# One gate pair computed plain inside the attention stage, attention operands formed three heads ahead, z's splits moved, scores and bias table negated

## The chip, the cores and the metric

The kernel runs on one core of a Trainium2 chip, in one launch. Its work is spread over TensorE (PE, matmuls into PSUM), VectorE (DVE), ScalarE (ACT), GpSimd (POOL) and SyncE (SP, which issues most DMAs); each engine takes its instructions in a fixed order, and waits on semaphores where it needs another's result. The metric is the device time of one execution in microseconds, the median over runs. Before the change it is 641.82 us (640.44 to 642.54 in 3 runs).

## The reference

One decoder layer on 512 tokens of 1024 channels, all in float32: a combined projection, a block-sparse attention with 8 heads of 64 channels and a bias by distance, a pooling mixer beside it, both merged by sigmoid gates, an output projection, a layer norm, a gated MLP with a short convolution, and another layer norm. The parts that the change touches:

```python
proj = h @ w_in[l]
q, k, v, p, g = jnp.split(proj, [ATTN_WIDTH, 2 * ATTN_WIDTH, 3 * ATTN_WIDTH, 3 * ATTN_WIDTH + POOL_WIDTH], axis=-1)
y_attn = moba_attention(q.reshape(hs), k.reshape(hs), v.reshape(hs), rel_bias) @ w_branch_attn[l]
y_pool = multiscale_pool(p, w_pool_group[l], pool_scale[l]) @ w_branch_pool[l]
gates = jax.nn.sigmoid(g.astype(jnp.float32)).astype(h.dtype).reshape(B, S, N_BRANCHES, D)
mixed = gates[:, :, 0] * y_attn + gates[:, :, 1] * y_pool
...
s_own = jnp.einsum('hqd,hkd->hqk', qc, k_own).astype(jnp.float32) * scale
s_own = jnp.where((d_own >= 0)[None], s_own + bias_own, NEG)
...
p = jax.nn.softmax(logits, axis=-1).astype(v.dtype)
```

With 512 tokens and blocks of 256 every block is chosen, so the attention is plain causal attention.

## The kernel before

*Products.* A float32 product is made of three matmuls on operands that are split in two rounded parts: high x high, high x low, low x high (L249). `split` (L73) makes the high part on ScalarE (L77) and the low part on VectorE (L78). Weights come as chunks of 128 x 1024 by DMA on SyncE (`fetch`, L138) and are split into a ring of five slots; `state["limit"]` says how far the fetching may run ahead.

*Pairs of tiles by seven products.* Two output tiles of 128 channels that share their input are computed by a scheme with seven block products instead of eight (`seven`, L296). Its weight chunks are A, X, D and Y, of which X and Y are sums: X is formed by a DMA that adds in memory (L201), Y on VectorE (L215). The last product of a pair (`close`, L313) is put off until the next pair runs `flush`. In this way are made the pool projection and the four q/k pairs (key "i", 0 to 4), the eight gate pairs (key "g", one tile for each branch) and most of the MLP (key "f"). A tile made without it, by 24 matmuls of 512 columns, is called plain here (`in_tile`, L490).

*Attention.* `head(h)` (L436) forms a head's operands: a copy of k and of q with their rounding remainders on ScalarE and VectorE, and then SyncE sends the two k tiles to the other half of the partitions (L453, tiles k and kl). `scores(h)` (L535) multiplies them (tile sc, L546 and L547), adds the bias strip and takes the running maximum on VectorE (L550, a reduction into nm), negates nm (L553), exponentiates on ScalarE (L556), and multiplies by the reciprocal of the sums on GpSimd (L561). `trans(h)` (L622) transposes the probabilities on TensorE (tile tr) and copies them out of PSUM, and `pv(p)` (L637) multiplies two heads with v (tile ob). The bias strips are read from a table in memory that `make_table` (L383) and `write_end` (L403) fill.

*Fillers.* Between the steps of the heads TensorE does the products of the pool branch, br with z as input: `br_mm(h, 1)` in the loop over heads (L654 to L667), one for each of heads 0 to 6. They need z's splits (L651), which stand ahead of the loop. `head(h + 3)` is put behind the softmax of head h + 1. Then come the products of the attention branch (`BR0`), the eight gate pairs (L732), which `gate_done` multiplies into the branch products, and the output projection.

*Order.* The order within each engine is made by a scheduler when the program is built, from the order of the code and estimates; `tc.issue_after(ins)` puts what is written under it behind `ins` on that instruction's own engine, and on no other. PSUM has eight banks, each reused when its last reader has run.

## Time and profile before

| | before |
|---|---|
| median of 3 runs | 641.82 us (640.44 to 642.54) |
| profiled execution | 642.55 us |
| its span, first to last instruction | 640.5 us |
| mean granted TensorE clock | 0.985 |
| attention stage (first scores to the last value product) | about 76 to 161 us |
| gate pairs | 174 us to about 252 us |

The span is what the trace covers; 2.05 us of the profiled execution lie around it. In the views that follow, a row of a timeline has the start and the length in us, the engine, the line of the kernel, the operation, the tile written and the tiles read (without their numbers), and in brackets the idle time of that engine ahead of it with what ended it. The letters in tile names: sa, sb and sc with i, g or f are the PSUM banks of a seven-product pair; sc alone is a head's scores; whi and wlo are the two parts of a weight chunk. A matmul's length overlaps with the next one's start, so the distance of two starts tells its cost. A row of waits has engine, line and tile, what was waited for, and the us in total, the times and the longest.

### The profile page before, as it was taken

How to read it: one execution, taken by the hardware profiler on the slowest of the kernel's cores; microseconds unless marked ns; L12 is line 12 of the kernel's file. 1: busy time of each engine (PE TensorE's matmuls, PEld its weight loads, DVE VectorE, ACT ScalarE, POOL GpSimd, SP SyncE). 2: the span in 40 equal slices, each digit the busy share in tenths (PEclk: the TensorE clock that was granted, in tenths of full speed). 3: DMA queues.
4: the chain of work that ended last, by engine and by line, in shares of the span. 5: the costliest groups of instructions: out<-in, count | busy, mean ns of one | idle time of the engine just before them, and what ended most of it. 6: DMA issues, size and time to landing. Idle time of an engine off the chain costs nothing.

```text
span 640.5 us, 10780 instructions
## 1 busy us (share of the span) xinstructions
PE 622.2 (97%) x4132; PEld 560.3 (87%) x4132; DVE 518.0 (81%) x800; ACT 364.9 (57%) x560; POOL 117.7 (18%) x131
## 2 busy tenths in 40 slices
PE   9999989889999999999999999999999999999994
PEld 6899978666899999888999999999999888888884
DVE  6978778563779998749898888899897959698596
ACT  6646667563566565604576666567656447555352
POOL 0133133433012211210102010111100202123202
PEclk9999997889999999999999999999999999999998
DMA  8567645335377844551828877777753995899905
GB/s 315 157 187 185 173 124 166 99 98 165 99 211 183 212 119 131 178 218 45 252 84 203 192 197 197 173 194 198 185 141 117 324 271 118 207 205 201 267 2 131
DMA packets 44259, 110.87 MB, mean 173 GB/s; under 512 B 4512, under 2 KB 6824, under 8 KB 43952
## 3 DMA queue, kind: packets, MB, share of 16 engines
q1 hardware_dynamic: 30464, 75.05, 35.0%
q0 software_dynamic: 13168, 34.10, 28.5%
q10 hardware_dynamic: 576, 1.05, 0.4%
q8 instruction: 32, 0.52, 0.3%
q14 instruction: 19, 0.16, 0.1%
HBM read 104.91 MB, written 3.17 MB: 169 GB/s over the span
## 4 chain that ended last, share of the span: by engine, by line
PE 90%; DMA 5%; DVE 2%; ACT 1%; issue 1%; SPq 0%; DVEq 0%; ACTq 0%; POOLq 0%
PE saf L255 5%; PE saf L251 5%; PE saf L254 5%; PE v L428 3%; PE fi L251 3%; PE fi L254 3%; PE fi L255 3%; PE sbf L255 2%; PE sbf L251 2%; PE sbf L254 2%; PE sag L251 2%; PE wo L255 2%; PE wo L254 2%; PE wo L251 2%; PE sag L254 2%; PE sag L255 2%
## 5 line engine op out<-in xcount | busy, mean ns | idle before, releaser
L78 DVE TENSOR_TENSOR wlo<-araw,whi 128x1024 fp32r<-128x1024 f32 x60 | 72.8, 1222 | 6.7 <-ACT whi L77 6.0
L77 ACT ACTIVATE whi<-araw 128x1024 fp32r<-128x1024 f32 x60 | 62.7, 1057 | 20.4 <-PE sag L254 6.2
L77 ACT ACTIVATE whi<-wraw 128x1024 fp32r<-128x1024 f32 (+1 forms) x45 | 45.1, 1016 | 38.8 <-DMA wraw<-in_w_fo 10.9
L78 DVE TENSOR_TENSOR wlo<-wraw,whi 128x1024 fp32r<-128x1024 f32 (+1 forms) x45 | 53.3, 1192 | 16.8 <-ACT whi L77 16.6
L201 POOL DMA_DIRECT2D xraw<-in_w_fi x15 | 18.0, 1203 | 137.4 <-DMA xraw<-in_w_fi 54.4
L77 ACT ACTIVATE whi<-tw 128x1024 fp32r<-128x1024 f32 (+1 forms) x30 | 29.4, 983 | 23.5 <-DMA tw<-in_w_fo 10.4
L78 DVE TENSOR_TENSOR wlo<-tw,whi 128x1024 fp32r<-128x1024 f32 (+1 forms) x30 | 33.3, 1125 | 7.1 <-ACT whi L77 7.1
L255 PE MATMUL sbf<-T_hi,wlo 128*128 128x256 f32 x136 | 37.9, 279 | 0.0
L251 PE MATMUL saf<-hT_hi,whi 128*128 128x256 f32 x136 | 37.8, 278 | 0.0
L255 PE MATMUL saf<-nT_hi,wlo 128*128 128x256 f32 x136 | 37.8, 278 | 0.0
L254 PE MATMUL saf<-nT_lo,whi 128*128 128x256 f32 x136 | 37.8, 278 | 0.0
L251 PE MATMUL sbf<-T_hi,whi 128*128 128x256 f32 x136 | 37.7, 278 | 0.0
L254 PE MATMUL sbf<-T_lo,whi 128*128 128x256 f32 x136 | 37.7, 277 | 0.0
L254 PE MATMUL saf<-hT_lo,whi 128*128 128x256 f32 x136 | 37.7, 277 | 0.0
L251 PE MATMUL saf<-nT_hi,whi 128*128 128x256 f32 x136 | 37.7, 277 | 0.0
L255 PE MATMUL saf<-hT_hi,wlo 128*128 128x256 f32 x136 | 37.7, 278 | 0.0
L251 PE MATMUL fi<-hT_hi,whi 128*128 128x256 f32 (+1 forms) x112 | 36.2, 328 | 0.2 <-ACT hT_hi L77 0.2
L254 PE MATMUL fi<-hT_lo,whi 128*128 128x256 f32 (+1 forms) x112 | 36.4, 327 | 0.0
L255 PE MATMUL fi<-hT_hi,wlo 128*128 128x256 f32 (+1 forms) x112 | 36.3, 326 | 0.0
L561 POOL TENSOR_SCALAR pp<-pp,rs 128x128 f32<-128x128 f32 (+3 forms) x32 | 24.6, 784 | 23.0 <-DVE rs L558 19.0
L239 POOL DMA_DIRECT2D tw<-in_w_fo x18 | 15.6, 895 | 59.8 <-DVE wlo L78 59.8
L254 PEld LDWEIGHTS saf<-hT_lo,whi 128*128 128x128 f32 x136 | 25.5, 188 | 0.0
(338 smaller groups left out, 2249.9 us busy)
## 6 DMA issues: line engine op xcount, KB each, us to landing
tw<-in_w_fo POOLq DMA_DIRECT2D x20, 512.0 KB, 8.9
araw<-in_w_fi SPq DMA_DIRECT2D x17, 512.0 KB, 3.9
xraw<-in_w_fi SPq DMA_DIRECT2D x15, 512.0 KB, 4.3
xraw<-in_w_fi POOLq DMA_DIRECT2D x15, 512.0 KB, 6.6
araw<-in_w_c SPq DMA_DIRECT2D x13, 512.0 KB, 4.3
wraw<-in_w_fi SPq DMA_DIRECT2D x10, 512.0 KB, 4.4
wraw<-in_w_fo SPq DMA_DIRECT2D x10, 512.0 KB, 6.9
tw<-in_w_fo SPq DMA_DIRECT2D x10, 512.0 KB, 7.7
```

The lines of the kernel that those rows point to most:

```text
L77: state["hi"] = nc.scalar.activation(hi, src, AF.Copy)
L78: state["lo"] = nc.vector.tensor_tensor(lo, src, hi.bitcast(F32), op=ALU.subtract)
L201: state["acc"] = nc.gpsimd.dma_start(v, bass.AP(tensor=a.tensor, offset=a.offset, ap=[[pst, pn], [u.offset + S - a.offset, 2], [est, S]]), ...
L239: nc.gpsimd.dma_start(raw, half(then[1:], sl), accum_op=ALU.add)
L251: ins = nc.tensor.matmul(out_, wh, ah, start=start, stop=False, **kw)
L254: nc.tensor.matmul(out_, wh, al, start=False, stop=False, **kw)
L255: nc.tensor.matmul(out_, wl, ah, start=False, stop=stop, **kw)
L428: nc.tensor.matmul(bs[j], xs_[j][a], (wh, wl)[b], start=kt == 0 and n == 0, stop=False)
L561: nc.gpsimd.tensor_scalar(pp[:, offs[i]:offs[i] + n], pp[:, offs[i]:offs[i] + n], rs[:, i:i + 1], 1.0, op0=ALU.mult, op1=ALU.mult)
```

## The change

It does five things.

1. Gate pair 0 is no longer made by seven products. Its two tiles (g0 and g8) are plain, and they are made inside the attention loop, as the fillers of heads 0 and 1. VectorE copies them to a buffer `plain_gate`; their sigmoids, the multiplication with the branch products and the sum stand behind the first remaining gate pair.
2. The br products with z move back by two heads: filler h is br product h - 2, and one more filler stands behind the last head.
3. `head(h + 3)` is put behind the softmax of head h (of head 1 for the first), not of head h + 1.
4. z's splits move from ahead of the loop to behind head 0's round, and are held until the softmax of head 1.
5. The table of biases and its end are negated and k isn't, so that PSUM holds the scores with their sign turned: VectorE takes a minimum, which is the bias that the exponential needs, and the negation of nm falls away; the exponential gets a scale of -1.

```diff
-    for f in range(KT):
+    for j in (0, KT):
+        add(("g", j), w_c[first["g"] + j])
...
+    for f in range(1, KT):
         add_seven(("g", f), w_c[first["g"] + f], w_c[first["g"] + KT + f])
...
-            nc.vector.tensor_copy(F_sb[:H, S - lo_ - n:S - lo_],
-                                  bass.AP(tensor=rel.tensor, offset=at_, ap=[[pst, pn], [step, n]]))
+            nc.vector.tensor_scalar(F_sb[:H, S - lo_ - n:S - lo_],
+                                    bass.AP(tensor=rel.tensor, offset=at_, ap=[[pst, pn], [step, n]]), -1.0, None,
+                                    op0=ALU.mult)
...
-        nc.vector.memset(neg[:H, :STRIP - S], NEG)
+        nc.vector.memset(neg[:H, :STRIP - S], -NEG)
...
-            nc.scalar.activation(K1[h][own, :], kb[own, :], AF.Copy, scale=-1.0)
-            nc.vector.scalar_tensor_tensor(KL[h][own, :], kb[own, :], -1.0, K1[h][own, :].bitcast(F32),
-                                           op0=ALU.mult, op1=ALU.subtract)
+            nc.scalar.activation(K1[h][own, :], kb[own, :], AF.Copy)
+            nc.vector.tensor_tensor(KL[h][own, :], kb[own, :], K1[h][own, :].bitcast(F32), op=ALU.subtract)
...
-    state["limit"] = at["br", (2, 1)][0]
+    state["limit"] = at["g", KT]
...
-            nc.vector.tensor_tensor_reduce(out=pp[:, offs[i]:offs[i] + n], in0=dst[i][:, :n],
-                                           in1=strips[h][:, S - n:], scale=1.0, scalar=-3.0e38,
-                                           op0=ALU.add, op1=ALU.max, accum_out=nm[:, i:i + 1])
-        nms[h] = nc.vector.tensor_scalar(nm, nm, -1.0, None, op0=ALU.mult)
+            nms[h] = nc.vector.tensor_tensor_reduce(out=pp[:, offs[i]:offs[i] + n], in0=dst[i][:, :n],
+                                                    in1=strips[h][:, S - n:], scale=1.0, scalar=3.0e38,
+                                                    op0=ALU.add, op1=ALU.min, accum_out=nm[:, i:i + 1])
...
-                                           bias=nm[:, i:i + 1], accum_out=rs[:, i:i + 1])
+                                           scale=-1.0, bias=nm[:, i:i + 1], accum_out=rs[:, i:i + 1])
...
+    plain_gate = keep.tile([P, 2, S], F32, name="plain_gate")
...
-    for k in range(4):
-        split(zT_hi[:, k, :], zT_lo[:, k, :], zT[:, k, :])
-    turned = state["hi"].ins, state["lo"].ins
+
+    def cover(h):
+        if h < 2:
+            nc.vector.tensor_copy(plain_gate[:, h, :], in_tile("g", h * KT))
+        else:
+            f = h - 2
+            state["limit"] = at["br", (min(f + 3, KT - 2), 1)][0]
+            with tc.issue_after(turned[0]), tc.issue_after(turned[1]):
+                br_done(f, 1, br_mm(f, 1))
+
     for h in range(H):
         if h + 3 < H:
-            head(h + 3, nms[h + 1], exps[h + 1])
-        if h < KT - 1:
-            state["limit"] = at["br", (min(h + 3, KT - 2), 1)][0]
-            with tc.issue_after(turned[0]), tc.issue_after(turned[1]):
-                br_done(h, 1, br_mm(h, 1))
+            head(h + 3, nms[max(h, 1)], exps[max(h, 1)])
+        cover(h)
         if h + 2 < H:
             scores(h + 2)
...
             trans(h)
+        if h == 0:
+            state["limit"] = at["br", (2, 1)][0]
+            with tc.issue_after(nms[1].ins), tc.issue_after(exps[1].ins):
+                for k in range(4):
+                    split(zT_hi[:, k, :], zT_lo[:, k, :], zT[:, k, :])
+            turned = state["hi"].ins, state["lo"].ins
+    cover(H)
...
-    for f in range(KT):
+    for f in range(1, KT):
...
+        if f == 1:
+            with tc.issue_after(state["add"].ins):
+                for br in range(2):
+                    nc.scalar.activation(plain_gate[:, br, :], plain_gate[:, br, :], AF.Sigmoid)
+                    nc.vector.tensor_tensor(branch[0, br], branch[0, br], plain_gate[:, br, :], op=ALU.mult)
+            merged(0, branch[0, 0], branch[0, 1])
```

The rest of the diff swaps which of two buffers an even and an odd gate pair use.

What the scheduler makes of it stands in the order of the instructions. First TensorE around the first transposes of head 0, before (sai4 is the last q/k pair, br0_1 the first br product with z, sc2 the scores of head 2):

```order
L255 MATMUL sai4_968<-xT_hi_73,wlo25_973 128x256
L251 MATMUL br0_1_1163<-zT_hi_1086,whi26_1017 128x512
L546 MATMUL sc2_01_1182<-k1_2_1138,q1_2_1137 128x256
L547 MATMUL sc2_01_1182<-kl_2_1139,q1_2_1137 128x256
...
L547 MATMUL sc2_3_1184<-kl_2_1139,q1_2_1137 128x512
L630 MATMUL tr0_0_1208<-ident_174,pp0_939 128x128 x4
L630 MATMUL tr0_1_1209<-ident_174,pp0_939 128x128 x4
L630 MATMUL tr0_2_1210<-ident_174,pp0_939 128x128 x2
L254 MATMUL br0_1_1163<-zT_lo_1087,whi26_1017 128x512
```

and TensorE at the same transposes of the change (g8 is the second plain gate tile):

```order
L257 MATMUL sai4_967<-inT1_hi_89,wlo23_871 128x256
L549 MATMUL sc2_3_1187<-kl_2_1138,q1_2_1136 128x512
L632 MATMUL tr0_0_1210<-ident_174,pp0_939 128x128 x4
L632 MATMUL tr0_1_1211<-ident_174,pp0_939 128x128 x4
L632 MATMUL tr0_2_1212<-ident_174,pp0_939 128x128 x2
L253 MATMUL g8_1255<-xT_hi_73,whi27_1035 128x512
L256 MATMUL g8_1255<-xT_lo_74,whi27_1035 128x512
```

Before the transposes the whole last pair has run, and a br product with z stands around them; now the second gate follows, and the last part of the last pair (its close) comes behind 23 of that gate's 24 matmuls.

Second, VectorE from the weight chunk ahead of head 3's operands on, in the change (kl and q1 are a head's operands, pp with nm a reduction of its scores, rk3 and sai4 the additions that end the last q/k pair):

```order
L78 TENSOR_TENSOR wlo28_1245<-wraw28_1243,whi28_1244 128x1024
L308 TENSOR_TENSOR rk3_966<-rk3_966,sbi4_1000 128x256
L559 RECIPROCAL rs1_1097<-rs1_1097 128x4
L450 TENSOR_TENSOR kl_3_1147<-rk1_666,k1_3_1146 64x512
L452 SCALAR_TENSOR_TENSOR q1_3_1145<-rq1_851,q1_3_1145 64x4x128
L450 TENSOR_TENSOR kl_4_1236<-rk2_804,k1_4_1235 64x512
L452 SCALAR_TENSOR_TENSOR q1_4_1234<-rq2_1013,q1_4_1234 64x4x128
L552 ISA pp2_1182,nm2_1183<-sc2_01_1185,strip2_937 128x128
L552 ISA nm2_1183 128x1
L552 ISA pp2_1182,nm2_1183<-sc2_01_1185,strip2_937 128x256
```

Before, head 4's two rows stood behind the reductions of head 3, and the additions into sai4 stood ahead of head 3's operands; now head 4's rows are ahead of the reductions of head 2, and those additions follow behind them.

Third, ScalarE between the exponentials of heads 2 and 3, in the change (zT_hi are z's splits, PT0 and PT1 the copies of transposed probabilities, L754 the sigmoids of the plain gates):

```order
L634 ACTIVATE PT0_1209<-tr0_0_1210 128x512
L77 ACTIVATE zT_hi_1085<-zT_78 128x512 x4
L77 ACTIVATE whi30_1417<-wraw30_1416 128x1024
L754 ACT_TABLE_LOAD
L754 ACTIVATE plain_gate_1089<-plain_gate_1089 128x512
L77 ACTIVATE whi31_1561<-wraw31_1560 128x1024
L77 ACTIVATE whi32_1712<-wraw32_1711 128x1024
L529 ACTIVATE rq3_1134<-sai4_967 128x512
L754 ACTIVATE plain_gate_1089<-plain_gate_1089 128x512
L634 ACTIVATE PT1_1310<-tr1_0_1311 128x512
L557 ACT_TABLE_LOAD
L557 ACTIVATE pp3_1283,rs3_1285<-pp3_1283,nm3_1284 128x128
```

Before, z's splits stood ahead of the exponentials of head 2, and no table load stood in the attention stage behind the one for the first exponential; now the two sigmoids, each table loaded anew, are ahead of the exponentials of head 3.

## The prediction, made before the changed kernel was run

> **What bounds the kernel now.** I read the page first, then TensorE's waits, its timeline at those waits, and last the granted clock around them.

> ```profile
> span 640.5 us, 10780 instructions
> ...
> PE 622.2 (97%) x4132; PEld 560.3 (87%) x4132; DVE 518.0 (81%) x800; ACT 364.9 (57%) x560; POOL 117.7 (18%) x131
> ...
> PEclk9999997889999999999999999999999999999998
> ```

> TensorE is busy for 97% of the span, so a change pays only by less TensorE work, fewer of its waits, or a higher clock. A slice of the clock strip is 16 us long: the 7, 8, 8 are slices 7 to 9, from 96 to 144 us, the attention stage. What stands still there, the list of TensorE's waits tells:

> ```profile
> PE sc L546 <- DMA k<-k: 4.1, 2, 2.1
> PE sai L251 <- DVE sai L311: 2.4, 1, 2.4
> ...
> PE br L251 <- ACT zT_hi L77: 1.2, 1, 1.2
> PE sag L251 <- ACT quad L304: 0.4, 1, 0.4
> ```

> The timeline of TensorE places them; the bracket is the idle time ahead of a row:

> ```profile
> 94.91 0.39 PE L251 MATMUL sai<-xT_hi,whi 128*128 128x256 f32 x1 [2.39 <-DVE sai L311]
> ...
> 98.27 0.79 PE L251 MATMUL br<-zT_hi,whi 128*128 128x512 f32 x1 [1.18 <-ACT zT_hi L77]
> ...
> 115.65 0.77 PE L546 MATMUL sc<-k,q 128*128 128x256 f32 x3 [2.10 <-DMA k<-k]
> ...
> 132.29 0.76 PE L546 MATMUL sc<-k,q 128*128 128x256 f32 x3 [1.99 <-DMA k<-k]
> ```

> The sum is 2.39 + 1.18 + 2.10 + 1.99 = 7.66 us. The last close of the q/k projections waits for VectorE, the first filler product waits for z's splits, and the scores of heads 4 and 6 wait for the copy of k into the other half of the partitions. A wait costs more than its length, as the windows behind each show (length, TensorE busy, granted clock):

> ```profile
> 94.90:103.30 8.40, 7.22 (x33) 0.59 0.41 111
> 115.60:121.20 5.60, 5.55 (x27) 0.70 0.46 141
> 132.20:138.20 6.00, 5.91 (x29) 0.72 0.23 51
> 140.00:190.00 50.00, 50.00 (x309) 1.00 0.54 150
> ```

> The clock is halved for a while, and then full again. Lost are 8.40 x 0.41 = 3.44, less half of the 1.18 us that were idle anyway (0.59), so 2.85; then 5.60 x 0.30 = 1.68 and 6.00 x 0.28 = 1.68: together **6.2 us**. [...]

> **The change, part by part.** *Work on TensorE.* Gate pair 0 loses its seven products (84 matmuls of 256 columns) and gets two plain tiles (2 x 24 of 512). Three starts in a row of full-clock work:

> ```profile
> 171.50 0.39 PE L251 MATMUL br<-oT_hi,whi 128*128 128x512 f32 x1
> ...
> 174.22 0.28 PE L251 MATMUL sag<-xT_hi,whi 128*128 128x256 f32 x1
> ...
> 177.00 0.28 PE L251 MATMUL sbg<-gT_hi,whi 128*128 128x256 f32 x1
> ```

> 12 matmuls of 512 columns start from 171.50 to 174.22, 0.2267 each; 24 of 256 from there to 177.00, 0.1158 each. 48 x 0.2267 - 84 x 0.1158 = 10.88 - 9.73 = **+1.15 us**.

> *The waits for k.* Head h+3 is formed behind the softmax of head h instead of h+1. In the trace head 4's k is copied behind head 2's last exp and sent on at once:

> ```profile
> 110.34 0.62 ACT L446 ACTIVATE k<-rk 64x512 fp32r<-64x512 f32 x1
> ```
> ```profile
> 110.98 0.47 SPq L453 DMA_DIRECT2D k<-k  x1
> ```

> Scores 4 started 115.65 - 110.34 = 5.3 us after that copy began. In the changed order k of head 4 comes behind the exps of head 1, near 97 in the walk below, and is wanted near 114. The lead grows from 5 to about 17 us, so both waits (4.09) and their clock (3.36) should go.

> *The first two waits.* The close that waited 2.39 for VectorE now stands behind 23 of the second gate's 24 matmuls, and z's first product behind two whole gates; their 3.57 us and the 2.85 of clock go, unless the same engines are late at a new place. To see that, I walk from 86.41, until where TensorE's order is the same, with these durations:

> ```profile
> 86.41 0.69 PE L546 MATMUL sc<-k,q 128*128 128x256 f32 x3
> ...
> 88.31 0.39 PE L255 MATMUL sai<-inT_hi,wlo 128*128 128x256 f32 x1
> ...
> 142.92 1.25 PE L630 MATMUL tr<-ident,pp 128*128 128x128 f32 x10
> ```
> ```profile
> 88.28 5.73 SPq L154 DMA_DIRECT2D wraw<-in_w_br  x3
> ```
> ```profile
> wraw<-in_w_br SPq DMA_DIRECT2D x8, 512.0 KB, 4.1
> ```
> ```profile
> L556 ACT ACTIVATE pp<-pp,nm 128x128 f32<-128x128 f32 (+3 forms) x28 | 15.4, 553 | 8.2 <-DVE nm L553 8.2
> L77 ACT ACTIVATE whi<-wraw 128x1024 fp32r<-128x1024 f32 x7 | 7.1, 1047 | 3.1 <-PE br L254 3.1
> ```
> ```profile
> L550 DVE CUSTOM_DVE_ANT_0 pp<-sc,strip 128x128 f32<-128x128 f32 (+3 forms) x28 | 12.4, 485 | 7.5 <-issue 6.8 <-PE sc L547 0.5
> L78 DVE TENSOR_TENSOR wlo<-wraw,whi 128x1024 fp32r<-128x1024 f32 x7 | 9.1, 1294 | 0.1
> L450 DVE SCALAR_TENSOR_TENSOR q<-rq,q 64x512 fp32r<-64x512 f32 x6 | 4.9, 812 | 0.2
> L447 DVE SCALAR_TENSOR_TENSOR kl<-rk,k 64x512 fp32r<-64x512 f32 x6 | 4.2, 693 | 1.8 <-ACT k L446 1.8
> ```

> **Place one, the second gate.** TensorE has 36 small matmuls (4.2), the first gate (5.4), scores 1 and 2 in pieces (1.6 each: 88.31 - 86.41, less two strays) and ten transposes (1.0): it is there at 86.4 + 13.8 = 100.2. A PSUM bank makes it wait for VectorE's third reduction of head 2. That chain starts with the load of chunk 28, issued behind VectorE's split of chunk 25: 88.28 before, say 88.7 now, since a 0.81 us operand of head 2 goes ahead of it and head 0's softmax ends earlier. It lands 4.1 later, 92.8. ScalarE's split stands in the middle of head 1's exps: 1.05, then three exps 1.66, a 256-column copy 0.4, k 0.6: 96.5. VectorE: head 3's and 4's operands 2 x (0.69 + 0.81) = 3.0, three reductions 1.3: 100.8. **TensorE waits 0.6.**

> **Place two, the first z product.** From 100.8 TensorE has a gate 5.4, a close 1.4, scores 1.3 and transposes 1.0: 109.9. It needs the bank that VectorE frees by copying the second gate. Ahead of that stand, end to end, two splits of 1024 columns (2.6), a reduction and two half adds (1.5), head 5's operands (1.5), four z splits (2.9), a reciprocal and four PSUM copies, the two gates' and head 0's (2.6): 11.1, or 111.9. VectorE's rows overlap, though:

> ```profile
> 101.74 0.68 DVE L78 TENSOR_TENSOR zT_lo<-zT,zT_hi 128x512 fp32r<-128x512 f32 x1
> 102.34 0.68 DVE L550 CUSTOM_DVE_ANT_0 pp<-sc,strip 128x512 f32<-128x512 f32 x1
> ```

> 0.60 apart for 0.68, so some 14 rows save 1.1: a wait of 0.9. New waits: 0.6 + 0.9 = **+1.5 us**. Bounds: nothing (both chains are within 1 us of TensorE), and at the other end two waits as long as the longest shown, 2 x 2.39, each with 1.68 of clock: 8.1. I take 1.5 without clock, being nearer to the 0.4 us wait on the list, which left the strip at 9, than to 1.99.

> *Sigmoids.* The hold on the plain gates' sigmoids is an instruction of VectorE, so ScalarE's order is free of it, and they stand ahead of head 3's exps, with a table load on either side. A load's row, and the sigmoid behind it:

> ```profile
> 185.76 1.28 ACT L718 ACT_TABLE_LOAD   x1
> 187.06 0.63 ACT L718 ACTIVATE quad<-quad 128x512 f32<-128x512 f32 x1
> ```

> ScalarE gets 2 x 1.28 + 2 x 0.63 = 3.8 us there. By its queue from head 2's exps (near 104) to head 3's: three copies 1.8, four z splits 2.5, three weight splits 3.1, rq and a PSUM copy 1.2, the 3.8, less overlaps of some 1.3, then four exps 2.2: 117.3. Head 3's reciprocal leads VectorE's second reduction of head 4 (0.4), for whose bank the second z product waits; TensorE gets there at 110.8 + 2.7 + 1.3 + 2.4 + 1.0 = 118.2. Hidden, by 0.5 us only; at full price 3.8. [...]

> *The rest.* The last pair's value product is no longer torn apart:

> ```profile
> 146.85 2.38 PE L643 MATMUL ob<-PT,vv 128*64 128x512 f32 x16
> ...
> 153.11 1.07 PE L643 MATMUL ob<-PT,vv 128*64 128x512 f32 x2
> ...
> 158.41 2.37 PE L643 MATMUL ob<-PT,vv 128*64 128x512 f32 x14
> ```

> 1.07 + 2.37 - 2.38 = **-1.06 us**. The dropped negation of nm, the sign in the table and in exp, and k's plain copy are as many rows or fewer on engines that TensorE doesn't wait for now; at nothing, hidden by the fillers, between -1 and +0.5. From the second gate pair on every engine's order is as before, one pair shorter, so the 0.4 us wait there stays; -0.4 to +1.4, as VectorE gets two multiplies (0.69 each in rows of their kind) beside it.

> Sum: -7.66 - 6.2 - 1.06 + 1.15 + 1.5 = **-12.3 us**. The profiled execution took 642.55 (span 640.5 and 2.05 around it), so 630.3; the median of the runs is 0.73 below it, hence **629.6 us**.

> **Rivals.** (1) *Short waits halve the clock too.* No row shows a lone wait between 0.4 and 1.99, so the threshold is open. One or both new waits add 1.68 each: 631.3 to 633.0. (2) *Head 3 is late.* If each switch of tables cost twice its row, ScalarE would be 2 x 1.28 = 2.56 us later, the second z product would wait 2.56 - 0.5 = 2.1 and pay 1.68 of clock: 633.4. Against it: the sigmoid starts 0.02 us behind the load. [...] (3) *k stays late* for heads 4 and 6, behind other transfers on SyncE's queue: 4.09 + 3.36 remain, 637.1. Against it: 17 us of lead. (4) *VectorE becomes the pace of a head: slower.* It has, per head, reductions 1.94, operands 1.50, PSUM copies 1.09, reciprocal 0.17, half of an oT split 0.34 and of a weight split 0.65: 5.7 us. TensorE has 2.7 + 1.0 + 1.3 + 1.2 = 6.2. Stretched by a tenth or more, VectorE makes TensorE wait at a bank in each of seven heads; if each wait costs the clock as well, 0.7 + 1.68 = 2.4 a head and 16.7 in all: 646.3. It decides from (12.3 + 1.9) / 7 = 2.0 us a head. Against it: rows overlap, so 5.7 is nearer 5.0, and the windows of before show no such bank wait. (5) *The gain is given back* in the gate stage, by transfers that collide: within 0.3%, near 641.

> **How the numbers follow.** Forecast 0.56, (1) 0.20, (2) 0.09, (3) 0.05, (4) 0.05, (5) 0.05. The low end has no new wait (-1.5) and scores that no longer run in pieces with loose ends in four heads (-1.6): 626.5. The high end has both new waits at their bound, 629.6 - 1.5 + 8.1 = 636.2, so 636.0; that takes in (1) and (2) and leaves out (3) to (5). Faster by more than 0.3% (1.9 us, about what a measurement can tell from no change) are the forecast and (1) to (3): 0.90; same 0.05; slower 0.05.

> **What would show it.** Right: no wait of scores for k; the list of TensorE's waits adds up to 3 us or less before 200 us; the clock strip has 9 from 96 to 144; the first product of gate pair 1 starts near 171.5, as 174.22 + 9.73 - 12.3. Wrong: a halved clock behind a wait under 1 us (1), a wait at a br product near 118 (2), k on the list (3), a wait in every head for VectorE (4), a gate stage longer than seven times 9.73 (5).

## The result, and the profile after

| | before | changed |
|---|---|---|
| median of four runs each | 641.68 us (640.44 to 642.54) | 630.54 us (629.33 to 630.67) |
| profiled execution, its span | 642.55 us, 640.5 | 630.66 us, 628.9 |
| first scores to first product of the output projection | 182.93 us | 171.67 us |

The ratio is 0.9824 [0.9803, 0.9844]; four more runs on another chip gave 629.81, against 641.16 in nine of the kernel before, 0.9825 [0.9808, 0.9842]. The forecast was 629.6.

The page and the list of TensorE's waits of the changed kernel, down to 0.7 us:

```profile
span 628.9 us, 10679 instructions
...
PE 615.4 (98%) x4096; PEld 556.1 (88%) x4096; DVE 516.7 (82%) x787; ACT 365.6 (58%) x557; POOL 115.9 (18%) x130
...
PEclk9999999999999999999999999999999999999998
```
```profile
PE br L253 <- DVE plain_gate L656: 1.4, 1, 1.4
PE tr L632 <- DVE nm L552: 1.3, 1, 1.3
...
PE sag L257 <- DVE wlo L78: 0.7, 1, 0.7
```

The four waits of the attention stage are gone, and with them the 7 and the two 8s of the clock strip. Two new ones stand at the two places that the walk named. TensorE's timeline of the changed kernel:

```profile
101.00 0.41 PE L632 MATMUL tr<-ident,pp 128*128 128x128 f32 x2 [1.31 <-DVE nm L552]
...
112.29 0.47 PE L253 MATMUL br<-zT_hi,whi 128*128 128x512 f32 x1 [1.36 <-DVE plain_gate L656]
...
172.24 0.28 PE L253 MATMUL sag<-xT_hi,whi 128*128 128x256 f32 x1
```
```profile
247.31 0.39 PE L253 MATMUL wo<-whi,mx_hi 128*128 128x512 f32 x1
```

and the last of these rows in the kernel before:

```profile
258.57 0.39 PE L251 MATMUL wo<-whi,mx_hi 128*128 128x512 f32 x1
```

In both profiles the first scores start at 75.64, so the row of wo gives a measure for the rest of this text, **the stretch**: from the first scores to the first product of the output projection, 258.57 - 75.64 = 182.93 before and 171.67 now. It leaves out the start of an execution (the first scores lie between 74.21 and 75.68 in the profiles below) and the MLP, and it repeats well where no clock is lost: 171.67 and 171.62 in two profiles of the changed kernel. But it is that of one execution. The profiled one of the kernel before took 642.55 us, more than any median of that kernel on record (640.16 to 641.82), and that of g1 below was its fastest (635.59, median 637.39). So a difference against 182.93 can be some us off (g1 is 6.78 us ahead by the stretch and 3.52 by the median), and the medians stand beside it.

### The profile page after: what moved, and what is told of

It reads as the page before. It is cut to its first block, busy times and chain, and to the rows that moved or that the text cites. A ratio compares the mean times of both kernels' runs of the same rounds, so it can differ in the third digit from the quotient of the medians.

```text
span 628.9 us, 10679 instructions
## 1 busy us (share of the span) xinstructions
PE 615.4 (98%) x4096; PEld 556.1 (88%) x4096; DVE 516.7 (82%) x787; ACT 365.6 (58%) x557; POOL 115.9 (18%) x130
## 3 DMA queue, kind: packets, MB, share of 16 engines
q10 hardware_dynamic: 576, 1.05, 0.4%
## 4 chain that ended last, share of the span: by engine, by line
PE 90%; DVE 5%; ACT 1%; issue 1%; DMA 1%; DVEq 0%; ACTq 0%
PE saf L253 5%; PE saf L257 5%; PE saf L256 5%; PE v L431 3%; PE fi L253 3%; PE fi L256 3%; PE fi L257 3%; PE sbf L253 3%; PE sbf L256 2%; PE sbf L257 2%; PE br L253 2%; PE br L256 2%; PE br L257 2%; PE wo L256 2%; PE wo L257 2%; PE wo L253 2%
## 5 line engine op out<-in xcount | busy, mean ns | idle before, releaser
L78 DVE TENSOR_TENSOR wlo<-araw,whi 128x1024 fp32r<-128x1024 f32 x58 | 71.1, 1233 | 7.8 <-ACT whi L77 7.4
L77 ACT ACTIVATE whi<-araw 128x1024 fp32r<-128x1024 f32 x58 | 60.7, 1059 | 23.1 <-PE saf L256 5.3
L78 DVE TENSOR_TENSOR wlo<-wraw,whi 128x1024 fp32r<-128x1024 f32 (+1 forms) x47 | 56.5, 1213 | 15.5 <-ACT whi L77 15.4
L77 ACT ACTIVATE whi<-wraw 128x1024 fp32r<-128x1024 f32 (+1 forms) x47 | 47.4, 1019 | 37.1 <-DMA wraw<-in_w_fo 10.4
L77 ACT ACTIVATE whi<-tw 128x1024 fp32r<-128x1024 f32 (+1 forms) x30 | 29.4, 984 | 22.8 <-DMA tw<-in_w_fo 9.3
L78 DVE TENSOR_TENSOR wlo<-tw,whi 128x1024 fp32r<-128x1024 f32 (+1 forms) x30 | 33.4, 1129 | 6.1 <-ACT whi L77 6.1
L562 POOL TENSOR_SCALAR pp<-pp,rs 128x128 f32<-128x128 f32 (+3 forms) x32 | 22.9, 730 | 19.2 <-DVE rs L559 14.0
## 6 DMA issues: line engine op xcount, KB each, us to landing
tw<-in_w_fo POOLq DMA_DIRECT2D x20, 512.0 KB, 8.2
araw<-in_w_fi SPq DMA_DIRECT2D x17, 512.0 KB, 4.4
xraw<-in_w_fi SPq DMA_DIRECT2D x15, 512.0 KB, 4.5
xraw<-in_w_fi POOLq DMA_DIRECT2D x15, 512.0 KB, 6.7
araw<-in_w_c SPq DMA_DIRECT2D x12, 512.0 KB, 3.8
wraw<-in_w_fi SPq DMA_DIRECT2D x10, 512.0 KB, 3.5
wraw<-in_w_fo SPq DMA_DIRECT2D x10, 512.0 KB, 7.1
tw<-in_w_fo SPq DMA_DIRECT2D x10, 512.0 KB, 7.5
```

The source lines that it names most:

```text
L77: state["hi"] = nc.scalar.activation(hi, src, AF.Copy)
L78: state["lo"] = nc.vector.tensor_tensor(lo, src, hi.bitcast(F32), op=ALU.subtract)
L562: nc.gpsimd.tensor_scalar(pp[:, offs[i]:offs[i] + n], pp[:, offs[i]:offs[i] + n], rs[:, i:i + 1], 1.0, op0=ALU.mult, op1=ALU.mult)
```

## The experiments

Medians are of four to seven runs, and ratios are against runs of the kernel before on the same chip. One more kernel, p_kl256 in the last part, ran once (630.35 us) and is used for its trace alone. Each edit also lets the scheduler make a new order on every engine, so a run tells what an edit does together with its order.

| kernel | median us | ratio [95%] | stretch us |
|---|---|---|---|
| before, operands early alone (e2) | 632.98 | 0.9874 [0.9856, 0.9892] | 174.45 |
| before, signs alone (n1) | 632.59 | 0.9873 [0.9837, 0.9909] | 175.37 |
| before, covers alone (g1) | 637.39 | 0.9948 [0.9931, 0.9965] | 176.15 |
| changed, operands late (e1) | 629.16 | 0.9820 [0.9800, 0.9840] | 169.94 |
| changed, old signs (e3) | 631.94 | 0.9861 [0.9839, 0.9883] | 172.93 |
| changed, sigmoids held (e4) | 630.37 | 0.9833 [0.9814, 0.9851] | 171.95 |
| changed, again (a1) | 629.81 | 0.9825 [0.9808, 0.9842] | 171.62 |
| changed, head 4 behind (e6) | 627.85 | 0.9796 [0.9779, 0.9813] | 169.65 |
| operands late, sigmoids and multiplications moved (c2) | 628.63 | 0.9825 [0.9798, 0.9853] | 168.96 |
| head 4 behind, sigmoids and multiplications moved (c4) | 628.02 | 0.9793 [0.9774, 0.9812] | 167.92 |
| head 4 behind, multiplications moved (d1) | 626.79 | 0.9789 [0.9760, 0.9818] | 167.88 |

### Which part removed the waits for k

Two runs take the early operands apart: the changed kernel without them, and the kernel before with nothing else.

```diff
-            head(h + 3, nms[max(h, 1)], exps[max(h, 1)])
+            head(h + 3, nms[h + 1], exps[h + 1])
```

> The changed kernel, but each head's operands are formed where they were before (head h+3 behind the softmax of head h+1). Theory L (the lead decides, 5.3 us from the start of k's copy to the scores, as in the kernel before): head 4's copy would start near 104.3 and is wanted at 115.1, no wait; head 5's near 118.1, wanted at 122.7, a wait of 0.7; head 6's near 122.4, wanted at 127.8, none; head 7's near 131.8, wanted at 135.4, a wait of 1.7. Together 2.4 us and no or one halved clock: 632.9 to 634.6. Rival K (the shift of the operands carries its whole term of the prediction, 4.09 + 3.36): 638.0. Rival G (the covers alone removed the waits): 630.5.

The second is the same edit the other way round, in the kernel before.

> The kernel before, with one edit of the change: head h+3 is formed behind the softmax of head h (of head 1 for the first). Theory L and K: k of heads 4 and 6 comes about a head earlier, both waits of scores for k (4.09) and the halved clock behind them (3.36) go, and the two first waits stay with theirs: 641.7 - 7.5 = 634.2, 633.5 to 635.0. Rival G: 641.7. In the list of waits no sc row, and 2.4 and 1.2 still there.

The waits of e1 and then of e2 between the first scores and the gate pairs, as their lists have them:

```profile
PE br L253 <- ACT rq L529: 1.0, 1, 1.0
```
```profile
PE br L251 <- ACT zT_hi L77: 2.7, 1, 2.7
PE sai L251 <- DVE sai L311: 2.4, 1, 2.4
```

Neither has a wait for k. In the kernel before the early operands do what the prediction says of them (632.98 where 634.2 was expected), but in the changed kernel k does not need them: without them it is no slower, and its stretch is 1.73 us shorter. Theory L was wrong about e1 by its two waits, theory K by all of its 7.45. Rival G came near e1's time (630.5 for 629.16), but it had none of e2's gain, and the run with the covers alone, below, speaks against its cause. So something else in the change gives k its lead too. It could be the covers or the signs.

```diff
-            nc.vector.tensor_tensor_reduce(out=pp[:, offs[i]:offs[i] + n], in0=dst[i][:, :n],
-                                           in1=strips[h][:, S - n:], scale=1.0, scalar=-3.0e38,
-                                           op0=ALU.add, op1=ALU.max, accum_out=nm[:, i:i + 1])
-        nms[h] = nc.vector.tensor_scalar(nm, nm, -1.0, None, op0=ALU.mult)
+            nms[h] = nc.vector.tensor_tensor_reduce(out=pp[:, offs[i]:offs[i] + n], in0=dst[i][:, :n],
+                                                    in1=strips[h][:, S - n:], scale=1.0, scalar=3.0e38,
+                                                    op0=ALU.add, op1=ALU.min, accum_out=nm[:, i:i + 1])
```

The signs (with the table, its end, k and the scale of the exponential, as in the change) were put back in the changed kernel (e3), and made alone in the kernel before (n1):

> The changed kernel, but the bias table, its end and the scores have their old signs again and nm is negated by a row of its own on VectorE (8 rows of 0.157). Theory: these rows are hidden except where VectorE is late (the two waits of 1.31 and 1.36): at most 2 x 0.16 more, 630.5 to 630.9. Rival: VectorE is the pace of every head, each row and its latency count: 630.5 + 8 x 0.16 = 631.8 or more.

> The kernel before, with one edit of the change: the bias table, its end and the scores negated, and no row that negates nm. Theory from the run with the old signs in the changed kernel: the edit's worth is not VectorE's 8 rows but TensorE's order, which the scheduler makes without torn transposes and value products: the last value product is whole again (1.06 us less), scores and transposes of heads 4 to 6 lose their loose ends; the four waits stay, perhaps 0.2 shorter: 1 to 3 us less than the kernel before. Rival (what the prediction said): nothing, -1 to +0.5. From the first scores to the first output-projection product: 180 to 182 by the theory, 182 to 183.4 by the rival (182.93 in the kernel before).

Both theories missed, and in one direction: the edit is worth more than either gave it. In e3 the rival's time came out (631.8 or more, and 631.94), but not its cause: the list of e3 has no wait in every head for VectorE. It has none of the changed kernel's two new waits either, but two others, of 0.8 and 0.6. In n1 the edit alone takes 7.6 us off the median, two and a half times the most that was expected. VectorE and then ScalarE around the softmax of head 2, in the kernel before:

```profile
100.11 0.28 DVE L550 CUSTOM_DVE_ANT_0 pp<-sc,strip 128x128 f32<-128x128 f32 x1
...
102.34 0.68 DVE L550 CUSTOM_DVE_ANT_0 pp<-sc,strip 128x512 f32<-128x512 f32 x1
...
102.95 1.21 DVE L78 TENSOR_TENSOR wlo<-wraw,whi 128x1024 fp32r<-128x1024 f32 x1
104.09 0.68 DVE L633 COPY PT<-tr 128x512 f32<-128x512 f32 x1
104.69 0.41 DVE L634 COPY PT<-tr 128x256 f32<-128x256 f32 x1
105.02 1.21 DVE L78 TENSOR_TENSOR wlo<-wraw,whi 128x1024 fp32r<-128x1024 f32 x1
106.15 0.15 DVE L553 TENSOR_SCALAR nm<-nm 128x4 f32<-128x4 f32 x1
```
```profile
106.34 0.40 ACT L556 ACTIVATE pp<-pp,nm 128x128 f32<-128x128 f32 x1 [2.76 <-DVE nm L553]
```

and with the signs alone:

```profile
100.37 0.29 DVE L550 CUSTOM_DVE_ANT_0 pp<-sc,strip 128x128 f32<-128x128 f32 x1 [1.66 <-PE sc L547]
```
```profile
100.71 0.40 ACT L555 ACTIVATE pp<-pp,nm 128x128 f32<-128x128 f32 x1 [0.24 <-DVE nm L550]
...
103.92 0.62 ACT L447 ACTIVATE k<-rk 64x512 fp32r<-64x512 f32 x1
```

The negation is a row of 0.15 us, but it needs all four reductions, and VectorE takes it behind two weight splits and two copies out of PSUM that the scheduler put ahead of it: 106.15, when the last reduction had ended at 103.02. Every exponential waits for it. Without it an exponential needs only its own reduction, and the first starts 0.34 us after the first reduction has begun instead of 6.23. Head 4's k is copied behind the last one, at 110.34 before and at 103.92 here (34.70 and 29.36 us behind the first scores), and the wait for k is gone.

The other part of the theory, that the new signs give an order without torn groups, holds only beside the covers. With the old signs (e3) two value products are torn again, ob0 of the first two heads and ob3 of the last two (two matmuls, then 14), each for about a microsecond:

```profile
113.07 1.07 PE L646 MATMUL ob<-PT,vv 128*64 128x512 f32 x2
114.94 2.37 PE L646 MATMUL ob<-PT,vv 128*64 128x512 f32 x14 [0.80 <-ACT PT L635]
```
```profile
152.39 1.07 PE L646 MATMUL ob<-PT,vv 128*64 128x512 f32 x2
...
154.05 2.37 PE L646 MATMUL ob<-PT,vv 128*64 128x512 f32 x14
```

But in n1, with the new signs and without the covers, the same two are torn too, ob0 into 6 and 10 matmuls and ob3 into 2, 4 and 10, of which these are the first:

```profile
145.26 1.07 PE L642 MATMUL ob<-PT,vv 128*64 128x512 f32 x2
...
148.79 1.07 PE L642 MATMUL ob<-PT,vv 128*64 128x512 f32 x4
```

ob3 is torn in e2 and in g1 as well. It is whole in the changed kernel and in e1, where the new signs and the covers stand together.

That leaves the covers for the waits for k. In g1 they are the only part of the change: early operands and new signs are both undone.

> The kernel before with the covers alone (gate pair 0 plain, z's splits and products moved), operands formed as before, signs as before. In the run with old signs and early operands head 2's exponentials ended at 110.2 and the scores of head 4 started at 111.7. Theory L (lead of 5.3 us): formed behind those exponentials, head 4's k would be there at 115.5, a wait of 3.8, and others behind it: 4 to 8 us of waits for k and one to two halved stretches, from the first scores to the first output-projection product 178 to 184. Rival G (the covers give the lead whatever else is done): no wait for k, 172 to 174, as in that run (172.93).

Its one wait for k, and the copy of head 4's k on ScalarE:

```profile
PE sc L548 <- DMA k<-k: 4.2, 1, 4.2
```
```profile
111.69 0.61 ACT L448 ACTIVATE k<-rk 64x512 fp32r<-64x512 f32 x1
```

The copy starts at 111.69 and the scores at 116.59, 4.9 us later: the lead decides, as theory L has it, and the wait is the 4.2 us that it put at 3.8. It was wrong in that the later heads wait no more, so the stretch is 176.15, between the two theories. Covers alone bring the least of the three parts. **The early operands or the new signs remove the waits for k, either of them alone**: a gain of about 7.5 us that is there once, though both bring it. (The two together without the covers were not tried.) With late operands there is little to spare, though: in e1 head 5's k is copied at 115.10 and its scores start at 120.05, 4.95 us later, about what g1 shows to be needed.

The covers' own work is the other pair of waits, in the last q/k pair and at the first product with z. e2, above, keeps 2.4 and 2.7 there. In n1 both stand in the last q/k pair:

```profile
PE sai L251 <- ACT rk L304: 2.3, 1, 2.3
PE sai L251 <- DVE sai L311: 2.1, 1, 2.1
```

g1 has none of the two, and e1 one of 1.0 at the first product with z.

### The new waits, and the sigmoids

```diff
-            head(h + 3, nms[max(h, 1)], exps[max(h, 1)])
+            head(h + 3, nms[2 if h == 1 else max(h, 1)], exps[max(h, 1)])
```

This puts only head 4's two rows on VectorE behind head 2's reductions (e6), beside a repeat of the changed kernel:

> The changed kernel, but head 4's operands come behind head 2's reductions instead of ahead of them. Theory: the wait of 1.3 at the transposes is the price of head 4's two rows on VectorE (0.96 + 1.07) ahead of those reductions and goes; the copy of the second gate now stands ahead of a weight split, so the second wait shrinks too: 1.3 to 2.7 us less than the changed kernel. Rival: VectorE is simply behind, and what is not waited at the transposes is waited at the first product with z: no change, within 0.4.

> The changed kernel itself, beside the next three on the same chip: 630.0, 629.3 to 630.7, with waits of 1.3 (transposes, for VectorE), 1.4 (first product with z, for the copy of the second gate) and 0.7 (second remaining stage of gates).

VectorE ahead of those reductions in the changed kernel, where the transposes wait until 101.00:

```profile
96.58 0.71 DVE L450 TENSOR_TENSOR kl<-rk,k 64x512 fp32r<-64x512 f32 x1 [0.47 <-ACT k L449]
97.31 0.77 DVE L452 SCALAR_TENSOR_TENSOR q<-rq,q 64x512 fp32r<-64x512 f32 x1
98.12 0.96 DVE L450 TENSOR_TENSOR kl<-rk,k 64x512 fp32r<-64x512 f32 x1
99.11 1.07 DVE L452 SCALAR_TENSOR_TENSOR q<-rq,q 64x512 fp32r<-64x512 f32 x1
100.21 0.29 DVE L552 CUSTOM_DVE_ANT_0 pp<-sc,strip 128x128 f32<-128x128 f32 x1
```

and in e6, with what is left of the waits:

```profile
96.47 0.77 DVE L452 SCALAR_TENSOR_TENSOR q<-rq,q 64x512 fp32r<-64x512 f32 x1
97.28 0.29 DVE L552 CUSTOM_DVE_ANT_0 pp<-sc,strip 128x128 f32<-128x128 f32 x1
```
```profile
108.88 0.47 PE L253 MATMUL br<-zT_hi,whi 128*128 128x512 f32 x1 [0.66 <-DVE plain_gate L656]
```

The first wait is the price of head 4's 0.96 and 1.07 us ahead of the reductions, and it goes. It isn't paid again later: the second gate's copy now stands ahead of a weight split, and its wait halves. Stretch 171.62 to 169.65, median 629.81 to 627.85.

The sigmoids were held in two ways. In e4 they are behind a row of ScalarE in the gate stage:

```diff
-            with tc.issue_after(state["add"].ins):
+            with tc.issue_after(state["add"].ins), tc.issue_after(state["hi"].ins):
```

> The changed kernel, with the plain gates' sigmoids held on ScalarE until the gate stage, so that the two table loads (1.28 each) leave the attention stage. Theory: they were hidden, since no product waits near 118 in the changed kernel; the two waits of 1.31 and 1.36 are VectorE's and stay: 630.5, within 0.4. Rival: they held up head 3, and through it all that follows: up to 2.56 less, 628.

The two waits stay at 1.3 and 1.4, and the stretch up to the first gate pair is the same to 0.1 us: the two table loads of 1.28 us each were hidden. In the gate stage the held sigmoids cost a wait of 0.3 for a weight split, which is the 0.28 of the stretch.

In c2 and c4 they stand behind the last exponential, and the plain gates' multiplications are on GpSimd:

```diff
-                    nc.vector.tensor_tensor(branch[0, br], branch[0, br], plain_gate[:, br, :], op=ALU.mult)
+                    nc.gpsimd.tensor_tensor(branch[0, br], branch[0, br], plain_gate[:, br, :], op=ALU.mult)
```

> The changed kernel with the operands formed where they were before, the plain gates' sigmoids held behind the last exponential (no table load between exponentials), and their multiplications on GpSimd. Theory: each of the waits left in the run with late operands has one cause that goes: the 1.0 for rq on ScalarE (the sigmoids and a table load stand ahead of it), the 0.8 in the gate stage (VectorE's two multiplications): 2.5 to 2.8 us less than the changed kernel. Rival: the next engine is as late as the one relieved (VectorE's copy of the second gate; the transfers of the gate stage): 1.0 less, what late operands alone gave.

> Head 4's operands behind head 2's reductions, the sigmoids behind the last exponential, the multiplications on GpSimd. Theory: all three waits go, 1.3 + 1.4 + 0.7 = 3.4 us less than the changed kernel, 3.0 to 3.6. Rival: as above, the waits only move, 1.3 less or nothing.

By the stretch the waits are worth what was expected (2.66 and 3.70 us less than a1, for 2.5 to 2.8 and 3.0 to 3.6), and the gate stage's wait is gone in both. By the median they don't: c2 ran from 627.11 to 632.07, shows nothing certain against the changed kernel, and has a wait of 1.2 for k again; in c4's profile 1.06 us came back in the MLP, between its first saf and its first foa product (226.52, 225.46 in a1), where ScalarE waits 3.82 us for a weight sum that POOL's queue adds in memory, and 1.87 in a1. TensorE's own list has 0.3 us there, so that this wait is the cause is likely and not shown. Last, the multiplications alone on top of e6:

> Head 4's operands behind head 2's reductions, and the plain gates' multiplications on GpSimd; sigmoids as in the changed kernel. Theory: the wait of 0.8 in the gate stage was VectorE's two multiplications and goes; the rest is as with head 4 alone: from the first scores to the first output-projection product 168.9 (169.65 there), about 627.1 if nothing is given back. Rival: the transfers of the MLP stage are late by as much, as in the run with all three edits, where 1.07 us came back between the first saf and the first foa product: 627.9 to 628.2.

Its first product with z waits 0.48 us, the gate stage not at all, and nothing comes back in the MLP (225.47). From the first remaining gate pair to the output projection it takes 73.44 us, 1.60 less than e6 (75.04), twice the wait that went; TensorE's order changes in that stage too, and the other half was not taken apart. The stretch is 167.88, and 626.79 is **the best time of the study**, 2.1% under the kernel before (0.9789 [0.9760, 0.9818]). It ran on another chip than a1; by the ratios the two intervals overlap, and e6 and c4 can't be told from it; by the stretch it is 3.74 us ahead of the changed kernel.

### How long a wait costs clock

```diff
+            if h == 4:
+                nc.vector.tensor_tensor(KL[h][own, :256], kb[own, :256], K1[h][own, :256].bitcast(F32), op=ALU.subtract)
             nc.vector.tensor_tensor(KL[h][own, :], kb[own, :], K1[h][own, :].bitcast(F32), op=ALU.subtract)
```

> The changed kernel with half of the row that forms head 4's kl done twice on VectorE, ahead of head 2's reductions, so that the wait at the transposes grows from 1.3 to about 1.8 us: a measurement of how long a lone wait of TensorE halves its granted clock (1.36 did not, 1.99 did). Theory A (the limit lies between 1.4 and 1.8): clock 0.5 for some 3 us behind it. Theory B (between 1.8 and 2.0): clock 1.0 throughout.

The wait:

```profile
100.75 0.41 PE L634 MATMUL tr<-ident,pp 128*128 128x128 f32 x2 [1.70 <-DVE nm L554]
```

It grew to 1.70 us and not to 1.8, and the clock stayed at 1.00 (100.50 to 103.90, in the last section). That speaks for theory B, though a limit between 1.70 and 1.8 is not excluded, and a wait of 2.40 us in e2 cost no clock (last section), so length alone does not decide it.

## Why the prediction was right, and where it was not

The total was right: 630.3 forecast for the profiled execution, 630.66 measured; 629.6 for the median, 630.54 measured. Its steps one by one:

- *The four waits and the halved clock gone* (-7.66, -6.2): right. The halved stretches of before, read at the edges, are 6.83 + 3.41 + 3.41 us; half of that, less half of the 1.18 us idle inside, is 6.24.
- *The waits for k go because head h+3 is formed a head earlier*: the row of waits is right, but **it is not the only cause** in the changed kernel. The mechanism (lead) is right: e2 shows the edit to be enough, and g1 shows the 4.9 us from copy to scores. But e1 shows that it isn't needed beside the new signs, and that it costs 1.73 us of stretch, since head 4's rows are what the transposes wait for.
- *"The dropped negation of nm ... at nothing"*: **the step that failed.** It was priced by its own 0.157 us rows, and they don't count. What counts is who waits for them. The row that said so stood in the prediction among the durations: the exponentials' group has 8.2 us of idle time, all put down to "DVE nm L553". Alone the edit is worth 7.6 us; undone in the changed kernel it costs 1.26 us of stretch, torn value products included. The sum came out because the gain that the signs make was already in it once, under the name of the early operands. In this the total was luck: the prediction didn't know that two of its parts bring the same gain.
- *Plain tiles +1.15, whole value product -1.06*: 23 products of the second gate take 5.36 us (101.39 to 106.75), 0.233 each where 0.227 was reckoned, and every ob group of the changed kernel runs whole, in 2.37 to 2.38 us. The prediction gave no edit for it. It takes two, the new signs and the covers: ob3 is torn in e3 and in n1, which each have only one of them.
- *New waits +1.5 at two places*: right in place and cause, too small, 1.31 + 1.36 = 2.67. At the first, TensorE was there at 99.7 and not 100.2, the four operand rows took 3.5 us and not 3.0, and by the times the bank came free with head 2's second reduction (its last row ends at 100.85), not with the third (101.33). At the second, TensorE was free at 110.9, a microsecond later than the walk has it, but the copy of the second gate ended at 112.15, where the walk has 110.8. VectorE started on that chain half a microsecond late, and most of the 1.1 us that overlapping rows should save was not there (10.8 us from the third reduction's end, for 11.1 less 1.1): the split just ahead of the copy took 1.63 us where 1.29 was reckoned.
- *Sigmoids hidden*: right (e4). *Gate stage -0.4 to +1.4*: right, a wait of 0.74 where 0.39 was before; the two multiplications are its cause, since it is gone in the three runs that move them (d1, c2, c4).

With these sizes the sum is -7.66 - 6.24 - 1.06 + 1.15 + 2.67 + 0.35 = -10.8; the stretch is 11.26 shorter. The remaining half microsecond may be what the low end named, scores that no longer run in pieces; it was not tried by itself. Of the signs of being right, one failed: TensorE's waits before 200 us were to add up to 3 us or less, and the three listed above alone add up to 3.41. The first product of gate pair 1 starts at 172.24, where 171.5 was named.

The rivals: (1), short waits that halve the clock, did not happen: behind the waits of 1.31 and 1.36 us the clock was 1.00. Nor did (2) to (5). That a switch of tables costs twice its row, as (2) supposes, no run shows: with both loads of 1.28 us moved to the gate stage (e4) the stretch up to the first gate pair is the same to 0.1 us, and in the changed kernel the next row starts 0.02 us behind a load. For (3), k late, g1 shows what it is like, though there the lead is missing and not a place on SyncE's queue: a wait of 4.2 us. For (4), VectorE as the pace of a head, there is no wait in every head in any list.

## What to carry to other kernels

Price a removed row by the queue in front of it and by who waits behind it, not by its own length: 0.15 us of negation stood 3 us behind the last reduction of head 2, and joined four reductions that could have been used one by one. When several edits of one change lengthen the same lead, count their gain once, and try each alone before keeping all: here the early operands, as they stand in the changed kernel, cost more stretch than they gave (the medians, 0.9820 without them and 0.9824 with them, don't tell them apart). Where an operand isn't needed for some 10 us, put it behind the row that the pacing engine waits for.

## What the runs showed of the hardware

In these runs the clock was halved for 3.41 or 6.83 us at a time. Windows of 3.4 us, laid at the edges, in the kernel before around the wait of 2.10 us, then in e2 around its waits of 2.40 (91.88 to 94.28) and 2.73 us (95.95 to 98.68), in the run with the longer wait, and in the changed kernel; columns are the window, its length, busy time and rows of PE, PEld, DVE, ACT and POOL, the granted clock, and the share and rate of DMA:

```profile
112.90:116.30 3.40, 1.30 (x6) 0.60 (x4) 1.87 (x4) 3.38 (x12) 3.15 (x4) 1.00 0.61 154
116.30:119.70 3.40, 3.40 (x11) 1.24 (x12) 1.50 (x2) 1.03 (x2) 2.63 (x4) 0.50 0.60 186
119.70:123.10 3.40, 3.40 (x27) 2.85 (x24) 1.44 (x7) 1.20 (x2) 0.00 (x0) 1.00 0.00 0
```
```profile
92.80:96.20 3.40, 1.67 (x12) 1.47 (x12) 1.56 (x6) 2.71 (x9) 0.12 (x1) 1.00 0.72 186
96.20:99.60 3.40, 0.92 (x6) 0.88 (x7) 3.06 (x4) 3.38 (x8) 3.32 (x4) 1.00 0.56 148
99.60:103.00 3.40, 3.40 (x16) 3.10 (x14) 3.37 (x11) 3.40 (x6) 0.00 (x0) 0.50 0.30 68
103.00:106.40 3.40, 3.40 (x17) 2.83 (x16) 3.40 (x6) 0.99 (x3) 0.58 (x1) 1.00 0.14 36
```
```profile
97.10:100.50 3.40, 1.95 (x17) 1.63 (x15) 3.31 (x7) 1.72 (x4) 1.70 (x2) 1.00 0.77 216
100.50:103.90 3.40, 3.15 (x14) 2.51 (x15) 3.37 (x10) 2.09 (x8) 0.45 (x1) 1.00 0.37 92
```
```profile
109.50:112.90 3.40, 2.04 (x15) 1.65 (x14) 3.40 (x8) 3.39 (x4) 0.97 (x1) 1.00 0.06 14
112.90:116.30 3.40, 3.40 (x19) 2.82 (x17) 3.40 (x7) 3.37 (x8) 0.58 (x1) 1.00 0.66 210
```
